# First products of the FFNs: eight column tiles with the tokens stationary, four of them as seven block products for eight

## The chip, the cores and the metric

The kernel runs on one core of a Trainium2 chip. Its engines work side by side: TensorE (in the profile PE, with its weight loads as PEld), VectorE (DVE), ScalarE (ACT), GpSimd (POOL) and SyncE (SP), which issues most transfers. The metric is the device time of one execution in microseconds, smaller being better.

## The reference

A bidirectional encoder trunk of two layers, with 256 tokens of width 1024 in float32. Each layer has a half-step feed-forward network (FFN), a mixer of two kinds of attention, and a second FFN. The change touches the FFNs alone.

```python
SEQ, D_MODEL, D_FF, DEPTH = 256, 1024, 2816, 2

def swiglu(x, w_in, w_out):
    h = x @ w_in
    gate, up = h[..., :D_FF], h[..., D_FF:]
    return (jax.nn.silu(gate) * up) @ w_out

for l in range(DEPTH):
    x = layer_norm(ALPHA * x + 0.5 * swiglu(x, ffn1_w_in[l], ffn1_w_out[l]), ln_g[l, 0], ln_b[l, 0])
    mix = hybrid_mixer(x, ...)
    x = layer_norm(ALPHA * x + mix, ln_g[l, 1], ln_b[l, 1])
    x = layer_norm(ALPHA * x + 0.5 * swiglu(x, ffn2_w_in[l], ffn2_w_out[l]), ln_g[l, 2], ln_b[l, 2])
```

## The kernel before, in words

**Numbers in two halves.** TensorE multiplies in a shortened float32 (fp32r). Each operand is therefore split in a high half (a cast, made on ScalarE: wh, L118) and a low half (the rest, a subtraction on VectorE: wl, L119). A product is then three: high by high, high by low, low by high. All weights come from memory and are split in the kernel. `Weights` does it in the order of a list, `srcs`: a tile of 128 x 1024 is loaded to `raw` (five buffers), and its halves go to `wh` and `wl` (nine buffers each). `W.get(i)` hands out entry i and emits what lies up to nine buffers ahead; that work has a priority of 100 places less (LATER).

**An FFN's first products (x @ w_in).** The width of 2816 is 22 column tiles of 128, each with a gate and an up half. x stands transposed in `xx`, in halves, with its 1024 channels as eight k tiles. Column tiles 0 to 3 (NB = 4) go through `first`: 128 tokens are stationary and 512 columns of weights move past them, for two token tiles, eight k tiles, three parts and two halves (gate, up): 96 matmuls of 512 columns (L381). Its results have the tokens on partitions; `first_t` (L397) transposes them with four TensorE transposes for each token tile, and splits them (L401, L402). The other 18 tiles go through `col`: the weights are stationary and all 256 tokens move, high and low half side by side, so for each half of a tile 8 "wide" matmuls of 512 columns (L419) with wh and 8 "narrow" ones of 256 (L424) with wl. ScalarE and VectorE then add the two parts of a bank (L434, L435), apply Silu (L436), multiply (L438) and split the product (L441, L442) into the tiles `gs`. Tiles come in twos; with `flip` the narrow matmuls go first.

**The second products.** The 22 row tiles of w_out are taken as "o" (one row tile, 12 matmuls, `step`, L503) or "S" (two row tiles as a block pair, `pair`, L527): 2 x 2 blocks are multiplied with seven products instead of eight, by sums of blocks (Winograd's form). The weight sums of a pair are made on VectorE in `_make_pair` (four operations, L86 to L89, before the splits, L72 and L73), those of the activations in `sums` (L457 to L462). `STR` names the five pairs, PLAN the order, and the last seven single tiles come at the end.

**Order.** TensorE's order is the order in which the program emits. The other engines' orders, and the buffers, are set by a scheduler when the kernel is built, by priority and its own estimate of times. PSUM has eight banks, all under one tag `b`.

**Stages in the profile.** FFNs begin at about 4.8, 283.3, 464.2 and 742.7 us; the mixers lie between the first and the second, and between the third and the fourth.

Of the kernel before, what the change touches and what calls it, by code (L numbers as in the profile page):

```python
# [19 lines left out]
P = 128  # L20
# [34 lines left out]
0; P sq 1 1; V 1; O 0 2; T sq 1; O 0 2; B 0 0; S s 1; B 0 1; Y 1; W 0 0; W 0 1; S s 1; O 1 1; O 0 1; O 1 1; O 0  # L55
3; B 1 0; B 1 1; W 1 0; W 1 1; O 1 2; Z; O 1 4
"""


class Weights:  # L60
# [15 lines left out]
    def _make_pair(self, i):  # L76


        nc, dv = self.nc, self.nc.vector
        r0, r1, ta = (self.pool.tile([P, 1024], F32, tag="raw", name=f"raw{i}{c}", bufs=5) for c in "abt")  # L80
        for r, src in zip((r0, r1), self.srcs[i][1:]):
            nc.sync.dma_start(r, src)
        t4 = self.tmp.tile([P, 512], F32, tag="tmp", name=f"t4_{i}")
        a, b = slice(0, 512), slice(512, 1024)
        with self.tc.high_priority(-LATER):
            dv.tensor_tensor(ta[:, a], r0[:, b], r0[:, a], ALU.subtract)  # L86
            dv.tensor_tensor(ta[:, b], r0[:, b], r1[:, b], ALU.add)
            dv.tensor_tensor(r0[:, b], r1[:, b], ta[:, a], ALU.add)
            dv.tensor_tensor(t4, r1[:, a], r0[:, b], ALU.subtract)  # L89
# [9 lines left out]
    def _make(self, i):  # L99
        nc = self.nc  # L100
        if self.srcs[i][0] == "S":
            return self._make_pair(i)
        raw = self.pool.tile([P, 1024], F32, tag="raw", name=f"raw{i}", bufs=5)
        wh = self.pool.tile([P, 1024], F32R, tag="wh", name=f"wh{i}", bufs=9)
        wl = self.pool.tile([P, 1024], F32R, tag="wl", name=f"wl{i}", bufs=9)

        n = 512 if i < 3 else 1024
        src = self.srcs[i]

        rows = src if isinstance(src, tuple) else (src,)  # L110
        for c in range(0, 1024, n):
            s = slice(c, c + n)
            for q, r in enumerate(rows):
                h = P // len(rows)

                (nc.sync if i or c else nc.scalar).dma_start(raw[q * h : (q + 1) * h, s], r[:, s])
            with self.tc.high_priority(0 if i < 3 else -LATER):
                nc.scalar.copy(wh[:, s], raw[:, s])  # L118
                nc.vector.tensor_tensor(wl[:, s], raw[:, s], wh[:, s].bitcast(F32), ALU.subtract)  # L119
        self.made.append((wh, wl))  # L120
# [15 lines left out]
def encoder_kernel(  # L136
# [44 lines left out]
    def out_rows(w):  # L181
        row = lambda k: w[k * P : (k + 1) * P, :]
        rows = [row(k) if u == "o" else ("S", row(2 * k), row(2 * k + 1)) for u, k in plan]
        return rows + [row(k) for k in tail]

    srcs = []
    for l in range(DEPTH):
        srcs += [f1_b[l, k] for k in range(KT)]
        srcs += [f1_in[l, j, s] for j in range(JT - NB) for s in range(2)]
# [9 lines left out]
        srcs += [f2_b[l, k] for k in range(KT)]  # L199
        srcs += [f2_in[l, j, s] for j in range(JT - NB) for s in range(2)]  # L200
        srcs += out_rows(f2_out[l])
    W = Weights(tc, wp, tp, srcs)
    wi = 0
# [113 lines left out]
        nc.sync.dma_start(bt, ln_b[l, n].partition_broadcast(P))  # L317
        return gt, bt

    def to_xt(src, t, nm, hs=(0, 1), gain=None):  # L320

        with tc.high_priority():
            for h in hs:
                tr = ps.tile([P, 4, P], F32, tag="b", name=f"tr_{nm}{t}{h}")
                for i in range(4):
                    c = (4 * h + i) * P
                    nc.tensor.transpose(tr[:, i, :], src[:, c : c + P], ident)
                dh = xx[:, 4 * h : 4 * h + 4, 0, t, :]
                dl = xx[:, 4 * h : 4 * h + 4, 1, t, :]
                if gain is None:  # L330
                    nc.scalar.copy(dh, tr)
                    dv.tensor_tensor(dl, tr, dh.bitcast(F32), ALU.subtract)
                else:
                    nc.scalar.mul(dh, tr, gain)
                    dv.scalar_tensor_tensor(dl, tr, gain, dh.bitcast(F32), ALU.mult, ALU.subtract)
# [25 lines left out]
    def ffn(l, n, last=False):  # L361
        nonlocal wi
        nm = f"{l}{n}"
        gs = [gp.tile([P, 2, 2, SEQ], F32R, tag="g", name=f"g_{nm}_{q}") for q in range(JT // 2)]

        def first(ts, mid=None):

# [23 lines left out]
                out.append(gv)  # L391
            return out

        def first_t(gv, t):
            tr = ps.tile([P, 4, P], F32, tag="b", name=f"trg_{nm}{t}")
            for i in range(4):
                nc.tensor.transpose(tr[:, i, :], gv[:, i * P : (i + 1) * P], ident)  # L397
            for q in range(2):
                a = slice(t * P, (t + 1) * P)
                dh = gs[q][:, :, 0, a]  # L400
                nc.scalar.copy(dh, tr[:, 2 * q : 2 * q + 2, :])  # L401
                dv.tensor_tensor(gs[q][:, :, 1, a], tr[:, 2 * q : 2 * q + 2, :], dh.bitcast(F32), ALU.subtract)  # L402

        def col(*js, flip=False):

            nonlocal wi
            ts = []
            for j in js:

                hs = [ps.tile([P, 2, SEQ], F32, tag="b", name=f"h{'gu'[s]}_{nm}_{j}") for s in range(2)]  # L410
# [5 lines left out]
            def wide(hs, ws, s):  # L416
                for k in range(KT):

                    mm(hs[s], ws[s][0][:, k * P : (k + 1) * P], xx[:, k], start=(k == 0 and not flip),  # L419
                       stop=(k == KT - 1 and flip), skip_group_check=flip)  # L420

            def narrow(hs, ws, s):
                for k in range(KT):
                    mm(hs[s][:, 1, :], ws[s][1][:, k * P : (k + 1) * P], xx[:, k, 0], start=(k == 0 and flip),  # L424
                       stop=(k == KT - 1 and not flip), skip_group_check=flip)

            one, two = (narrow, wide) if flip else (wide, narrow)
            for j, hs, tl, ws in ts:
                for s in range(2):
                    one(hs, ws, s)  # L430
            for j, hs, tl, ws in ts:
                for s in range(2):
                    two(hs, ws, s)
                    nc.scalar.copy(tl[:, s], hs[s][:, 1, :])  # L434
                    dv.tensor_tensor(tl[:, s], hs[s][:, 0, :], tl[:, s], ALU.add)  # L435
                nc.scalar.activation(tl[:, 0], tl[:, 0], AF.Silu)  # L436
                gv = tl[:, 1]
                dv.tensor_tensor(gv, tl[:, 0], gv, ALU.mult)  # L438
                q, jj = divmod(j, 2)
                n = P if q in STR and jj == 0 else SEQ  # L440
                nc.scalar.copy(gs[q][:, jj, 0, 0:n], gv[:, 0:n])  # L441
                dv.tensor_tensor(gs[q][:, jj, 1, 0:n], gv[:, 0:n], gs[q][:, jj, 0, 0:n].bitcast(F32), ALU.subtract)  # L442
                if q in STR and jj:
                    sums(q, ts[0][2][:, 1], gv)

        sm = {}

# [18 lines left out]
        if first_x:  # L466
            g0, g1 = first((0, 1))
        else:
            (g0,) = first((0,), lambda: to_xt(x[1], 1, f"x{nm}"))
            (g1,) = first((1,))  # L470
        wi += KT
        if not first_x:
# [89 lines left out]
        todo += [(i, [c]) for c in fin for i in range(TAIL - SPLIT, TAIL)]  # L562
        for n_, (i, cs) in enumerate(todo):
            if n_ == len(todo) - TCUT and not last:
                to_xt(x[0], 0, f"y{nm}")
# [18 lines left out]
    def mixer(l):  # L584
# [263 lines left out]
        for tok in ORDER.split(";"):  # L848
# [37 lines left out]
            elif op == "X":  # L886
                to_xt(x[1], 1, f"m{l}")
            elif op == "Z":
                to_xt(x[0], 0, f"z{l}")
            elif op == "S":  # L890
                do_s(*ar)
            elif op == "A":
# [89 lines left out]
```

## Time and profile before

| | |
|---|---|
| median of 3 runs | 931.92 us (931.63 to 932.51) |
| the profiled execution's own time | 931.88 us |
| its span in the profile | 930.1 us |
| granted TensorE clock, mean | 0.997 |
| PE busy | 922.0 us (99%), 4970 instructions |
| DVE busy | 789.5 us (85%), 1344 instructions |
| ACT busy | 569.1 us (61%), 970 instructions |
| HBM read | 174.35 MB, 189 GB/s over the span |

The span goes from the first to the last instruction that the profile counts. Busy is the share of the span in which an engine executes. The profile can be asked for the chain of work that ended last (followed back from the last instruction), for the busy time in chosen stretches, and for the instructions in order of time (start, duration, engine, line, operation, out<-in with sizes, count, and in brackets the idle time before with what ended it).

### The profile page before, as it was taken

Reading aid. Unit: us, or ns where it says so; the run is one execution under the profiler, and the core shown is the slowest. Engines: PE = TensorE matmul, PEld = TensorE weight load, DVE = VectorE, ACT = ScalarE, POOL = GpSimd, SP = SyncE. Lnnn points to the kernel's source line nnn. Section 1 sums busy time; section 2 is a strip of 40 time slices with the busy share of each in tenths; the row PEclk is TensorE's granted clock in tenths of the full one; section 3 lists DMA queues with packets and bytes.
Section 4 is the critical chain, followed back from the end, with each engine's and each line's share of the span. In section 5 each row is a group of like instructions: output and inputs, shape, how many; then the busy total and the mean of one; then the engine's idle time right before and its main releaser. Section 6 shows DMA issues by size and latency. Waiting matters only on the chain.

```text
span 930.1 us, 13767 instructions
## 1 busy us (share of the span) xinstructions
PE 922.0 (99%) x4970; PEld 788.2 (85%) x4970; DVE 789.5 (85%) x1344; ACT 569.1 (61%) x970; POOL 17.0 (2%) x27
## 2 busy tenths in 40 slices
PE   9999999999999999999999999999999999999996
PEld 7888888888888888888888888888888889888885
DVE  7898899998987678899986888999988976888896
ACT  5768656546865666656546666663478656666650
POOL 0000000000000000000000000000000000000000
PEclk9999999999999999999999999999999999999998
DMA  9986546675426755547675665575844365665551
GB/s 315 310 271 202 159 145 218 226 248 152 125 90 206 245 181 181 161 154 218 224 254 191 187 194 162 158 254 175 275 112 137 107 228 188 193 190 159 159 180 46
DMA packets 51379, 176.29 MB, mean 190 GB/s; under 512 B 6512, under 2 KB 8304, under 8 KB 51312
## 3 DMA queue, kind: packets, MB, share of 16 engines
q1 hardware_dynamic: 51024, 175.03, 58.7%
q8 instruction: 39, 0.64, 0.3%
q10 hardware_dynamic: 288, 0.39, 0.1%
q14 instruction: 28, 0.23, 0.1%
HBM read 174.35 MB, written 1.05 MB: 189 GB/s over the span
## 4 chain that ended last, share of the span: by engine, by line
PE 99%; DVE 1%; issue 0%; DVEq 0%
PE hg L419 14%; PE hu L419 14%; PE acc L503 14%; PE hb L381 9%; PE hu L424 7%; PE hg L424 7%; PE pp L527 6%; PE ao L840 5%; PE acc L527 4%; PE os L776 1%; PE pj_sq L619 1%; PE pj_sq L617 1%; PE pj_dv L617 1%; PE pj_sq L618 1%; PE pj_dq L617 1%; PE pj_dv L619 1%
## 5 line engine op out<-in xcount | busy, mean ns | idle before, releaser
L119 DVE TENSOR_TENSOR wl<-raw,wh 128x1024 fp32r<-128x1024 f32 (+1 forms) x279 | 336.1, 1210 | 73.7 <-PE hg L424 28.8
L118 ACT CAST wh<-raw 128x1024 fp32r<-128x1024 f32 (+1 forms) x279 | 290.6, 1047 | 117.4 <-PE acc L503 29.3
L419 PE MATMUL hg<-xx,wh 128*128 128x512 f32 x576 | 143.2, 391 | 0.0
L419 PE MATMUL hu<-xx,wh 128*128 128x512 f32 x576 | 142.3, 389 | 0.0
L419 PEld LDWEIGHTS hu<-xx,wh 128*128 128x128 f32 x576 | 108.1, 188 | 22.5
L419 PEld LDWEIGHTS hg<-xx,wh 128*128 128x128 f32 x576 | 106.6, 188 | 21.2
L503 PE MATMUL acc<-wh,g 128*128 128x512 f32 (+1 forms) x390 | 109.0, 387 | 0.0
L503 PEld LDWEIGHTS acc<-wh,g 128*128 128x128 f32 x390 | 72.9, 188 | 14.7
L424 PE MATMUL hg<-xx,wl 128*128 128x256 f32 x576 | 81.0, 283 | 0.0
L424 PE MATMUL hu<-xx,wl 128*128 128x256 f32 x576 | 80.9, 283 | 0.0
L424 PEld LDWEIGHTS hg<-xx,wl 128*128 128x128 f32 x576 | 75.4, 192 | 1.6
L424 PEld LDWEIGHTS hu<-xx,wl 128*128 128x128 f32 x576 | 74.3, 192 | 0.0
L381 PE MATMUL hb<-wh,xx 128*128 128x512 f32 x256 | 70.3, 395 | 0.0
L503 PE MATMUL acc<-wl,g 128*128 128x512 f32 (+1 forms) x195 | 61.6, 386 | 0.0
L381 PEld LDWEIGHTS hb<-wh,xx 128*128 128x128 f32 x256 | 48.3, 190 | 10.5 <-ACT wh L118 0.6
L434 ACT COPY tl<-hg 128x256 f32<-128x256 f32 x72 | 26.8, 372 | 32.0 <-PE hg L419 28.1
L503 PEld LDWEIGHTS acc<-wl,g 128*128 128x128 f32 x195 | 36.6, 188 | 7.3
L434 ACT COPY tl<-hu 128x256 f32<-128x256 f32 x72 | 26.8, 372 | 20.2 <-PE hu L424 17.1
L381 PE MATMUL hb<-wl,xx 128*128 128x512 f32 x128 | 38.9, 391 | 0.0
L840 PE MATMUL ao<-wh,xx 128*128 128x512 f32 x128 | 37.0, 398 | 0.0
L441 ACT CAST g<-tl 128x128 fp32r<-128x128 f32 (+1 forms) x72 | 27.1, 376 | 15.9 <-DVE tl L438 14.0
L436 ACT ACTIVATE tl<-tl 128x256 f32<-128x256 f32 x72 | 30.2, 419 | 6.5 <-DVE tl L435 5.6
(972 smaller groups left out, 1477.4 us busy)
## 6 DMA issues: line engine op xcount, KB each, us to landing
raw<-in_f_in_dram SPq DMA_DIRECT2D x144, 512.0 KB, 4.4
raw<-in_f_out_dram SPq DMA_DIRECT2D x48, 512.0 KB, 4.1
raw<-in_m_in_dram SPq DMA_DIRECT2D x36, 512.0 KB, 4.7
raw<-in_f_b_dram SPq DMA_DIRECT2D x29, 512.0 KB, 4.3
raw<-in_m_out_dram SPq DMA_DIRECT2D x8, 512.0 KB, 4.7
raw<-in_m_out_dram SPq DMA_DIRECT2D x16, 256.0 KB, 4.4
lng<-in_ln_g_dram SPq DMA_DIRECT2D x6, 512.0 KB, 4.9
lnb<-in_ln_b_dram SPq DMA_DIRECT2D x6, 512.0 KB, 6.0
```

Of the source, the lines that this page charges most:

```text
L118: nc.scalar.copy(wh[:, s], raw[:, s])
L119: nc.vector.tensor_tensor(wl[:, s], raw[:, s], wh[:, s].bitcast(F32), ALU.subtract)
L381: mm(hb[s], xx[:, k, g, t, :], ww[:, 512 * s : 512 * s + 512], start=(k == 0 and e == 0), stop=(k == KT - 1 and e == 2))
L419: mm(hs[s], ws[s][0][:, k * P : (k + 1) * P], xx[:, k], start=(k == 0 and not flip), stop=(k == KT - 1 and flip), skip_group_check=flip)
L424: mm(hs[s][:, 1, :], ws[s][1][:, k * P : (k + 1) * P], xx[:, k, 0], start=(k == 0 and flip), stop=(k == KT - 1 and not flip), skip_group_c ...
L434: nc.scalar.copy(tl[:, s], hs[s][:, 1, :])
L436: nc.scalar.activation(tl[:, 0], tl[:, 0], AF.Silu)
L441: nc.scalar.copy(gs[q][:, jj, 0, 0:n], gv[:, 0:n])
L503: mm(a, g, ww[:, s], start=(k == ka and e == 0), stop=(k == kb and e == 2))
L527: mm(o, g, ww, start=(own and first and e == 0), stop=(own and final and e == 2))
L617: mm(o, xx[:, k, 0, t, :], wh[:, s], start=(k == 0), stop=False)
L840: mm(acc[t][h], xx[:, k, g, t, :], ww[:, s], start=(k == 0 and e == 0), stop=(k == KT - 1 and e == 2))
```

## The change

NB goes from 4 to 8: column tiles 0 to 7 now have the tokens stationary. Tiles 0 to 3 (NF = 4) go through `first` as before. Tiles 4 to 7 go through the new `group`: two token tiles by two k tiles as 2 x 2 blocks, four such pairs of k tiles, seven products for each pair, each product in three parts, in seven banks: 84 matmuls of 512 columns. For it

- the weight tiles of the four pairs are made by `_make_pair` (through `S` entries in `srcs`, `in_rows`);
- x is needed unsplit: `to_xt` copies it to `xkeep` (on ScalarE, with a priority of KEEP = 20 places less), and the first FFN loads it from memory; `x_sums` makes four sums on VectorE and splits them;
- after each of the first three pairs, and after the banks are gathered, one half of the ordinary tiles 9 and 10 is computed (`by_halves`); tile 8 comes before the group through `col`;
- the seven banks are gathered to two results with VectorE and ScalarE, and `first_t` transposes these after column tile 11.

The pairs of the second products become 6 to 10 instead of 3 to 7. The tiles `gs` are allocated one by one. The loading of x and the rotary tables, in the first FFN, come after tiles 12 and 13 instead of 6 and 7. The weights of the first eight column tiles are laid out as 2048 columns for each k tile, of which an entry takes 512 gate and 512 up columns.

```diff
-NB = 4
+NF = 4
+KEEP = 20
+NB = 8
-STR = (3, 4, 5, 6, 7)
+STR = (6, 7, 8, 9, 10)
...
+    def in_rows(b, w):
+        blk = lambda g, k: b[k].rearrange("p (s g c) -> p g s c", s=2, g=NB // NF)[:, g]
+        cols = [w[j, s] for j in range(JT - NB) for s in range(2)]
+        mid = [u for k in range(KT // 2) for u in (("S", blk(1, 2 * k), blk(1, 2 * k + 1)), cols[2 + k])]
+        return [blk(0, k) for k in range(KT)] + cols[:2] + mid + cols[2 + KT // 2 :]
...
-    def to_xt(src, t, nm, hs=(0, 1), gain=None):
+    xkeep = {}
+
+    def to_xt(src, t, nm, hs=(0, 1), gain=None, keep=False):
...
+                    if keep:
+                        with tc.high_priority(-KEEP):
+                            nc.scalar.copy(xkeep[t][:, 4 * h : 4 * h + 4, :], tr)
...
+        def by_halves(*js):
+            nonlocal wi
+            for j in js:
+                tl = tp.tile([P, 2, SEQ], F32, tag="tl", name=f"tl_{nm}_{j}", bufs=2)
+                for s in range(2):
+                    h, w = bank(j, s), W.get(wi)
+                    wi += 1
+                    wide(h, w, False)
+                    narrow(h, w, False)
+                    gather(h, tl, s)
+                    if s:
+                        gated(j, tl)
+                    yield
...
+        def split(src, nm_):
+            s = gp.tile([P, 2, 4, P], F32R, tag="g", name=f"sx_{nm}_{nm_}")
+            nc.scalar.copy(s[:, 0], src)
+            dv.tensor_tensor(s[:, 1], src, s[:, 0].bitcast(F32), ALU.subtract)
+            return s
+
+        def x_sums():
+            v = [xkeep[t].rearrange("p (k e) c -> p k e c", e=2) for t in range(2)]
+            a11, a12, a21, a22 = v[0][:, :, 0], v[0][:, :, 1], v[1][:, :, 0], v[1][:, :, 1]
...
+            dv.tensor_tensor(s1, a21, a22, ALU.subtract)
...
+            dv.tensor_tensor(s4, a12, s2, ALU.subtract)
+            out.append(split(s4, 4))
+            return out
+
+        def group(xs, between):
+            nonlocal wi
+            b = {c: ps.tile([P, 512], F32, tag="b", name=f"pg_{nm}_{c}") for c in range(1, 8)}
+            for k in range(KT // 2):
+                b11, b21, b22, t4, t1, t2, t3 = W.get(wi)
+                wi += 1
...
+                for c in (2, 3, 5, 7, 1, 6, 4) if k < KT // 2 - 1 else (1, 2, 6, 7, 5, 3, 4):
+                    (ah, al), (bh, bl) = what[c]
+                    for e, (a_, w_) in enumerate(((ah, bh), (ah, bl), (al, bh))):
+                        mm(b[c], a_, w_, start=(k == 0 and e == 0), stop=(k == KT // 2 - 1 and e == 2))
+                if k < KT // 2 - 1:
+                    next(between)
...
+            nc.scalar.copy(v, b[1])
+            add(g0, b[2], v)
+            nc.scalar.activation(g0, g0, AF.Silu)
+            add(v, b[6], v)
+            add(w, b[7], v)
+            add(v, b[5], v)
+            add(u1, b[5], w)
+            add(v, b[3], v)
+            dv.tensor_tensor(v, g0, v, ALU.mult)
+            add(w, b[4], w)
+            nc.scalar.activation(w, w, AF.Silu)
+            dv.tensor_tensor(w, w, u1, ALU.mult)
+            next(between)
+            return v, w
...
+        if first_x:
+            for t in range(2):
+                xkeep[t] = gp.tile([P, KT, P], F32, tag="g", name=f"xf_{nm}{t}")
+                nc.sync.dma_start(xkeep[t], x_tr[:, t])
+        else:
             first_t(g0, 0)
+        xs = x_sums()
         col(NB)
...
-        for j in (NB + 1, *range(NB + 2, JT, 2)):
-
-            col(*((j,) if j == NB + 1 else (j, j + 1)), flip=(j % 4 == 0 or j == NB + 1))
-            if first_x and j == NB + 2:
+        ga, gb_ = group(xs, by_halves(NB + 1, NB + 2))
+        for j in (NB + 3, *range(NB + 4, JT, 2)):
+
+            col(*((j,) if j == NB + 3 else (j, j + 1)), flip=(j % 4 == 2 or j == NB + 3))
+            if j == NB + 3:
+                first_t(ga, 0, NF // 2)
+                first_t(gb_, 1, NF // 2)
+            if first_x and j == NB + 4:
```

More of the change, by code (lines that the diff above doesn't have):

```diff
@@ L57, with _cols @@
 """
+def _cols(t, like):
+    return t if len(like.shape) == 2 else t.rearrange("p (s c) -> p s c", s=like.shape[1])
 class Weights:
@@ L114, in _make @@
                 h = P // len(rows)
-                (nc.sync if i or c else nc.scalar).dma_start(raw[q * h : (q + 1) * h, s], r[:, s])
+                dst = _cols(raw[q * h : (q + 1) * h], r)
+                s_ = s if len(r.shape) == 2 else slice(c // 512, (c + n) // 512)
+                (nc.sync if i or c else nc.scalar).dma_start(dst[:, s_], r[:, s_])
             with self.tc.high_priority(0 if i < 3 else -LATER):
@@ L198, in encoder_kernel @@
                  for n in range(KT // 2)]
-        srcs += [f2_b[l, k] for k in range(KT)]
-        srcs += [f2_in[l, j, s] for j in range(JT - NB) for s in range(2)]
+        srcs += in_rows(f2_b[l], f2_in[l])
         srcs += out_rows(f2_out[l])
@@ L363, in ffn, with g_tiles @@
         nm = f"{l}{n}"
-        gs = [gp.tile([P, 2, 2, SEQ], F32R, tag="g", name=f"g_{nm}_{q}") for q in range(JT // 2)]
+        gs = {}
+        def g_tiles(*qs):
+            for q in qs:
+                gs[q] = gp.tile([P, 2, 2, SEQ], F32R, tag="g", name=f"g_{nm}_{q}")
         def first(ts, mid=None):
@@ L392, in first, with first_t @@
             return out
-        def first_t(gv, t):
-            tr = ps.tile([P, 4, P], F32, tag="b", name=f"trg_{nm}{t}")
+        def first_t(gv, t, q0=0):
+            if not t:
+                g_tiles(q0, q0 + 1)
+            tr = ps.tile([P, 4, P], F32, tag="b", name=f"trg_{nm}{t}{q0}")
             for i in range(4):
@@ L399, in first_t, with wide, narrow, gather @@
                 a = slice(t * P, (t + 1) * P)
-                dh = gs[q][:, :, 0, a]
+                dh = gs[q0 + q][:, :, 0, a]
                 nc.scalar.copy(dh, tr[:, 2 * q : 2 * q + 2, :])
-                dv.tensor_tensor(gs[q][:, :, 1, a], tr[:, 2 * q : 2 * q + 2, :], dh.bitcast(F32), ALU.subtract)
+                dv.tensor_tensor(gs[q0 + q][:, :, 1, a], tr[:, 2 * q : 2 * q + 2, :], dh.bitcast(F32), ALU.subtract)
+        def wide(h, w, flip):
+            for k in range(KT):
+                mm(h, w[0][:, k * P : (k + 1) * P], xx[:, k], start=(k == 0 and not flip),
+                   stop=(k == KT - 1 and flip), skip_group_check=flip)
+        def narrow(h, w, flip):
+            for k in range(KT):
+                mm(h[:, 1, :], w[1][:, k * P : (k + 1) * P], xx[:, k, 0], start=(k == 0 and flip),
+                   stop=(k == KT - 1 and not flip), skip_group_check=flip)
+        def gather(h, tl, s):
+            nc.scalar.copy(tl[:, s], h[:, 1, :])
+            dv.tensor_tensor(tl[:, s], h[:, 0, :], tl[:, s], ALU.add)
+        def gated(j, tl, prev=None):
+            nc.scalar.activation(tl[:, 0], tl[:, 0], AF.Silu)
+            gv = tl[:, 1]
+            dv.tensor_tensor(gv, tl[:, 0], gv, ALU.mult)
+            q, jj = divmod(j, 2)
+            if not jj:
+                g_tiles(q)
+            n = P if q in STR and jj == 0 else SEQ
+            nc.scalar.copy(gs[q][:, jj, 0, 0:n], gv[:, 0:n])
+            dv.tensor_tensor(gs[q][:, jj, 1, 0:n], gv[:, 0:n], gs[q][:, jj, 0, 0:n].bitcast(F32), ALU.subtract)
+            if q in STR and jj:
+                sums(q, prev[:, 1], gv)
+        def bank(j, s):
+            return ps.tile([P, 2, SEQ], F32, tag="b", name=f"h{'gu'[s]}_{nm}_{j}")
+        def by_halves(*js):
[11 more added lines that the diff above has]
+                    yield
         def col(*js, flip=False):
@@ L408, in col @@
             for j in js:
-                hs = [ps.tile([P, 2, SEQ], F32, tag="b", name=f"h{'gu'[s]}_{nm}_{j}") for s in range(2)]
+                hs = [bank(j, s) for s in range(2)]
                 tl = tp.tile([P, 2, SEQ], F32, tag="tl", name=f"tl_{nm}_{j}", bufs=2)
@@ L414, in col @@
                 ts.append((j, hs, tl, ws))
[L416 to L425, printed above, removed]
             one, two = (narrow, wide) if flip else (wide, narrow)
@@ L429, in col @@
                 for s in range(2):
-                    one(hs, ws, s)
+                    one(hs[s], ws[s], flip)
             for j, hs, tl, ws in ts:
                 for s in range(2):
[L433 to L444, printed above, removed]
+                    two(hs[s], ws[s], flip)
+                    gather(hs[s], tl, s)
+                gated(j, tl, ts[0][2])
+        def split(src, nm_):
[3 more added lines that the diff above has]
+            return s
@@ L468, in ffn @@
         else:
[L469 removed]
+            (g0,) = first((0,), lambda: to_xt(x[1], 1, f"x{nm}", keep=True))
             (g1,) = first((1,))
         wi += KT
[L472 removed]
+        if first_x:
+            for t in range(2):
+                xkeep[t] = gp.tile([P, KT, P], F32, tag="g", name=f"xf_{nm}{t}")
+                nc.sync.dma_start(xkeep[t], x_tr[:, t])
+        else:
             first_t(g0, 0)
+        xs = x_sums()
         col(NB)
```

27 lines of the change are left out of this document (22 added, 5 removed).

## The prediction

> **What bounds the kernel now.** I read the page's busy shares and its chain first, then the busy time by stage, then the chain and VectorE's timeline around the first products.
>
> ```profile
> PE 922.0 (99%) x4970; PEld 788.2 (85%) x4970; DVE 789.5 (85%) x1344; ACT 569.1 (61%) x970; POOL 17.0 (2%) x27
> PE 99%; DVE 1%; issue 0%; DVEq 0%
> ```
>
> TensorE is busy for 99% of the span, and the chain that ends last is 99% TensorE: a matmul less is time less, as long as what feeds TensorE keeps up. VectorE is next, with 85%. The shares by stage tell more (the columns: stretch and length, then busy us and count for PE, PEld, DVE, ACT and POOL, granted clock, DMA share, GB/s):
>
> ```profile
> 4.77:27.57 22.80, 22.80 (x98) 18.80 (x98) 18.64 (x25) 13.96 (x17) 0.00 (x0) 1.00 0.99 352
> 283.31:306.42 23.11, 23.11 (x109) 19.24 (x109) 17.13 (x22) 11.80 (x14) 1.00 (x1) 1.00 0.67 221
> 306.42:340.00 33.58, 33.58 (x196) 29.80 (x196) 24.23 (x43) 21.17 (x40) 0.00 (x0) 1.00 0.62 203
> 340.00:406.83 66.83, 66.83 (x386) 59.25 (x386) 55.42 (x102) 43.31 (x78) 0.00 (x0) 1.00 0.55 167
> 406.83:444.23 37.40, 37.40 (x167) 30.97 (x166) 34.35 (x39) 23.32 (x27) 0.00 (x0) 1.00 0.67 210
> ```
>
> The three middle rows are the first products of the second FFN: 123.5 us, in which VectorE works 17.13 + 24.23 + 55.42 = 96.8 us (78%) and ScalarE 76.3 us (62%). The last row is its second products with the five block pairs, where VectorE is at 92% and TensorE still never waits. The first row is the start of the first FFN, where the DMA engines are at 0.99. So the change is to be weighed on two accounts: what TensorE saves, and whether VectorE's slack of 26.7 us in those 123.5 us covers what it is given.
>
> **TensorE's account.** From the chain (start, length, what):
>
> ```profile
> 33.11 0.87 PE trg L397 x8
> 54.48 1.84 PE hg L419 x8
> 76.69 1.84 PE hg L419 x8
> 413.63 2.72 PE pp L527 x12
> 438.79 2.04 PE acc L527 x9
> 487.30 1.85 PE hg L419 x8
> 492.90 0.44 PE trg L397 x4
> ```
>
> Four ordinary column tiles go from 54.48 to 76.69, 22.21 us, so a half (gate or up of one tile) is 2.78 us. Their replacement is 4 pairs x 7 products x 3 = 84 matmuls of 512 columns. Such matmuls run at 2.72 / 12 = 0.2267 us each in the block pairs of the second products, so 19.04 us, one pair being 4.76. Two more sets of four transposes, 0.44 each, add 0.88. Net: 22.21 - 19.04 - 0.88 = 2.29 us saved in each FFN, 9.2 us in four. The eight tiles that now go tokens-stationary replace nothing else: first() keeps its 96 matmuls, and the two tiles that are split into halves run the same 32 each.
>
> **VectorE's account.** Its records overlap, so I price an operation by the distance between starts:
>
> ```profile
> 397.14 0.42 DVE L438 TENSOR_TENSOR tl<-tl 128x256 f32<-128x256 f32 x1
> 397.48 1.22 DVE L73 TENSOR_TENSOR wl133t<-raw133t,wh133t 128x1024 fp32r<-128x1024 f32 x1
> 428.16 0.69 DVE L86 TENSOR_TENSOR raw140t<-raw140a 128x512 f32<-128x512 f32 x1
> 428.76 0.69 DVE L73 TENSOR_TENSOR wl139f<-t,wh139f 128x512 fp32r<-128x512 f32 x1
> 429.36 0.69 DVE L87 TENSOR_TENSOR raw140t<-raw140a,raw140b 128x512 f32<-128x512 f32 x1
> 430.69 1.22 DVE L73 TENSOR_TENSOR wl140b<-raw140b,wh140b 128x1024 fp32r<-128x1024 f32 x1
> 431.82 0.68 DVE L89 TENSOR_TENSOR t<-raw140b,raw140a 128x512 f32<-128x512 f32 x1
> 511.71 0.28 DVE L459 TENSOR_TENSOR sf<-tl 128x128 f32<-128x128 f32 x1
> 511.91 0.28 DVE L457 TENSOR_TENSOR sf<-tl,tl 128x128 f32<-128x128 f32 x1
> ```
>
> 512 columns cost 0.605 us, 1024 cost 1.135, 256 cost 0.335, 128 cost 0.20. Removed in each FFN: 8 low halves of weights (9.1) and four tiles' two adds, product and subtraction (16 x 0.335 = 5.4), 14.5 in all. Added: 4 weight pairs, each five operations of 512 and three of 1024 = 6.43 (25.7); the x sums, four and their four low halves (4.8); the nine operations that gather the seven banks (5.4); four subtractions behind the new transposes (1.3): 37.3. Net +22.8 us in each FFN. The stage's account becomes 119.6 us of VectorE in 121.2 us of TensorE. Over the run VectorE goes from 789.5 to about 881 us, 95% of 923.
>
> [...]
>
> ```profile
> L118 ACT CAST wh<-raw 128x1024 fp32r<-128x1024 f32 (+1 forms) x279 | 290.6, 1047 | 117.4 <-PE acc L503 29.3
> ```
>
> ScalarE: the casts of a pair are three of 1024 and one of 512 against two of 1024 before, with x splits, x copies and two Silu; at 1.05 us per 1024 that is some 9 us on 76.3, 70%. It stays off the path. The x copies sit behind the casts of xx; the two loads of x for the first FFN move 1 MB, 3.0 us at 352 GB/s, on the sync queue behind weights. Weight rows in pieces of half the length: no row prices it; between 0 and the 1.05 us by which the first 96 matmuls (22.80) already exceed 96 x 0.2267. I take 0, as the rows after the start show DMA shares of 0.55 to 0.67. The moved block pairs of the second products, the tiles allocated late and the later rotary work cost TensorE nothing by themselves.
>
> **Where the slack is not.** An average of 119.6 in 121.2 us says little, since only nine weight buffers let VectorE run ahead. So I follow it from the point where it is first free for the new work:
>
> ```profile
> 18.53 6.35 DVE L119 TENSOR_TENSOR wl<-raw,wh 128x1024 fp32r<-128x1024 f32 x5
> 412.24 0.69 DVE L87 TENSOR_TENSOR raw137t<-raw137a,raw137b 128x512 f32<-128x512 f32 x1 [0.33 <-DMA raw137b<-in_f_out_dram]
> 421.68 0.69 DVE L87 TENSOR_TENSOR raw139t<-raw139a,raw139b 128x512 f32<-128x512 f32 x1 [0.50 <-DMA raw139b<-in_f_out_dram]
> 473.44 1.29 DVE L332 TENSOR_TENSOR xx<-tr_x,xx 128x512 fp32r<-128x512 f32 x2
> 476.42 0.69 DVE L390 TENSOR_TENSOR gvb<-sgb,hb 128x512 f32<-128x512 f32 x1 [1.68 <-ACT sgb L388]
> 507.19 1.23 DVE L119 TENSOR_TENSOR wl<-raw,wh 128x1024 fp32r<-128x1024 f32 x1 [5.23 <-issue]
> ```
>
> In a later FFN (the third) it is free at 474.7, with the eight rows' weights made. The group starts after the first column tile and g1's transposes, at 492.90 + 0.44 = 493.3. Ahead of it stand: two gate products 1.2, x sums 4.8, one column half 1.1, pair 0 6.4, eight operations of 256 for transposes and that tile 2.7, the next half 1.1: 17.4. The last pair begins three times (4.76 + 2.78) = 22.6 us into the group, at 515.9, and at once wants all but the last piece of its weights; for that VectorE needs pairs 1 and 2, two halves, 5.8 of pair 3 and the gathering of three halves, 22.6. It arrives at 474.7 + 40.0 = 514.7: 1.2 us early. Column tile 11 starts with the low halves of its weights, the second due at 515.9 + 7.54 + 0.95 = 524.4; by then come 10.5 more (the gathering of the banks 5.4, three weights 3.4, pair 3's rest and one half 1.6), until 525.2: 0.8 late, without a moment idle. The bank gathering is emitted ahead of those weights, so I let it go first.
>
> VectorE is not without idle time even when it is the busy one: 0.33 and 0.50 us before each pair's second row of weights, 8% in the stage of 37.40 us. On 50 us I allow 0 to 4 per cent, 0 to 2 us: late by 0.8 to 2.8, taken in the middle, 1.8, in each of three FFNs.
>
> In the first FFN it is free later relative to TensorE: the five operations from 18.53 end at 24.9, the last being for a weight that now comes after the pair, so 23.75. The DMA engines, full until 27.57, allow nothing earlier. The group would start at 33.11 + 0.87 = 34.0. Its work ahead is 16.3 (no first column halves), so the last pair's weights are ready at 23.75 + 38.9 = 62.7 against 56.6, 6.1 late; tile 11's at 73.1 against 65.1, 8.0 late. I take the middle, 7.0.
>
> Sum against the profiled execution, 931.88 us (0.04 below the median of the runs): -9.2 + 7.0 + 3 x 1.8 = +3.2, so 935.1. What is late next: nothing behind tile 11, where an ordinary tile needs two low halves, four operations of 256 and half a set of sums, 4.3 us of VectorE in 22.21 / 4 = 5.55, and it catches up.
>
> **The rivals.** First, on the other side: *the cover holds*. Place: the gathering of the banks against tile 11's weights. For it: 5.23 us in which VectorE stood still in the third FFN (507.19) and 1.68 before 476.42, and several counted operations that TensorE doesn't need yet (gatings, late transposes, some 2 us). If the weights go ahead of the gathering, only the last pair decides: it is early in three FFNs and 6.1 late in the first, 931.9 - 9.2 + 6.1 = 928.8; with everything hidden 922.7. It decides as soon as all stalls together stay under 9.2 us. Against it: the first FFN, where VectorE has hardly a gap.
>
> Second: *the backlog reaches the second products*. The last block pair there starts at 438.79 + 3 x 0.2267 = 439.5 and its first weights were done at 431.9, 7.6 us ahead. Three more sets of sums now fall into the last tiles (four operations of 128 columns and one of 512, 1.4 us each set), leaving 3.3. An arrears above that stops TensorE again, some 2 us in each FFN: 943.
>
> [...]
>
> **How the numbers follow.** About 0.2%, 1.9 us, is what a measurement here can tell from no change. VectorE late as summed, 933.8 to 942: 0.40. The cover holds, below 930: 0.37. Stalls that just eat the gain, 930 to 933.8: 0.17. The backlog in the second products or the slow clock: 0.06. So faster 0.37, same 0.17, slower 0.46. The predicted time is 935.1. The range leaves out full hiding at its low end and 943 and more at its high end: 925.5 to 942; the forecast's own is 933.8 to 942.
>
> **What would show it.** Matmuls of the group at 0.227 us where they run; VectorE's share near 95% overall and with almost no idle time from the second row of first() to tile 11; TensorE waiting on a weight's low half in the last pair or at tile 11, longest in the first FFN; no wait in the second products. I am wrong if TensorE stays without gaps in the group (then 922.7), or if the waits stand before the group, on the x sums or a bank.

## The result, and the profile after

The change makes the kernel slower: 947.82 us (median; 946.65 to 950.26) against 931.91 us, a ratio of 1.0175 (95% interval 1.0162 to 1.0187). The forecast was 935.1 with a range to 942.0: the sign is right, the size is not. The profiled execution took 946.83 us, and on it the rest of this section rests. Its page begins:

```profile
span 945.0 us, 13662 instructions
...
PE 922.1 (98%) x4826; PEld 778.7 (82%) x4826; DVE 868.2 (92%) x1460; ACT 593.5 (63%) x994; POOL 17.0 (2%) x27
...
PE 78%; DVE 13%; DMA 5%; ACT 2%; issue 2%; SPq 0%; DVEq 0%; ACTq 0%
```

TensorE has 144 instructions less and is busy just as long: its matmuls take longer somewhere. The chain, which was TensorE for 99%, now goes through VectorE for 13%. The chain also gives the borders of the stages (start, length, what): the first products of an FFN begin with `hb`, its second products with `acc` x24. In the chain of the kernel before, the second FFN begins at 283.31, and the third has:

```profile
464.19 8.17 PE hb L381 x36
...
587.72 5.44 PE acc L503 x24
```

The chain of the kernel after, with the second FFN's begin and the third's group:

```profile
294.09 8.16 PE hb L405 x36
...
475.39 8.17 PE hb L405 x36
...
508.07 5.54 PE pg L535 x16
...
516.39 4.79 PE pg L535 x21
...
601.02 5.47 PE acc L622 x24
```

From the one start to the other, the first products of the three later FFNs took 123.52, 123.53 and 123.53 us before; after, 123.92, 125.63 and 125.39. The second FFN begins 10.78 us later. Together 10.78 + 0.40 + 2.10 + 1.86 = 15.1 us. The row at 508.07 shows one reason: 16 matmuls in 5.54 us, where the whole pairs run 21 in 4.79 (0.228 each, as forecast). The waits of PEld in the changed kernel (us in total, times, longest), without those that the kernel before has too:

```profile
PEld pg L535 <- ACT sx L498: 10.0, 4, 3.1
PEld tr_y L343 <- DVE x L374: 2.8, 2, 2.6
...
PEld pg L535 <- DVE wl16a L79: 2.2, 1, 2.2
...
PEld pg L535 <- ACT wh16a L78: 1.6, 1, 1.6
```

`sx` are the split x sums: TensorE waits for them at the start of the group in all four FFNs (for 2.72, 1.85, 1.95 and 1.71 us on its own timeline, PE). Only in the first FFN does it wait for the last pair's weights (16a). Nothing waits at column tile 11.

The slow matmuls are seen in stretches laid behind these waits (stretch, length, busy us and count of PE, PEld, DVE, ACT and POOL, granted clock, DMA share, GB/s), in the changed kernel:

```profile
38.30:41.70 3.40, 3.37 (x8) 2.67 (x9) 3.40 (x8) 1.65 (x5) 0.00 (x0) 0.53 0.40 146
65.40:68.80 3.40, 3.40 (x8) 2.72 (x9) 2.48 (x4) 1.88 (x4) 0.00 (x0) 0.50 0.87 288
327.00:330.40 3.40, 3.40 (x16) 2.81 (x15) 3.40 (x7) 2.84 (x5) 0.00 (x0) 1.00 0.00 0
509.10:512.50 3.40, 3.40 (x9) 2.63 (x8) 3.40 (x6) 2.87 (x4) 0.00 (x0) 0.50 0.03 6
```

The stretches are the first FFN's group start and last pair, and the group starts of the second and third. In three of these four (0.53, 0.50 and 0.50), and in the fourth FFN (0.57 from 789.5 us), the clock is granted at half for about 3.4 us, and 8 to 10 matmuls run where 16 do at full clock; each time some 1.7 us are lost, an estimate from these rows (half of 3.4). Behind the wait of the second FFN it stays at 1.00.

Three of the waits ahead of such stretches, and in the third row one more wait, on the timeline of TensorE in the changed kernel (in brackets the idle time before and what ended it):

```profile
37.45 0.50 PE L535 MATMUL pg<-wh10b,sx 128*128 128x512 f32 x1 [2.72 <-ACT sx L498]
...
65.36 0.79 PE L535 MATMUL pg<-wl16a,xx 128*128 128x512 f32 x1 [1.88 <-DVE wl16a L79]
...
193.09 1.32 PE L343 MATMUL tr_y<-ident,x 128*128 128x128 f32 x8 [2.13 <-DVE x L374]
...
507.18 0.50 PE L535 MATMUL pg<-wh150b,sx 128*128 128x512 f32 x1 [1.95 <-ACT sx L498]
```

The third row is a wait that the forecast didn't have: behind the first FFN's second products, the transposes of the layer norm's result. Behind it the clock stays at 1.00 (193.00 to 197.80 us). Ahead of the second row TensorE had already waited 1.41 us for the same pair's high half, with three matmuls in between.

### The profile page after: what moved, and what is told of

Same layout as the page of the kernel before. It is cut to its first block, busy times and chain, and to the rows that moved or that the text cites. A ratio compares the mean times of both kernels' runs of the same rounds, so it can differ in the third digit from the quotient of the medians.

```text
span 945.0 us, 13662 instructions
## 1 busy us (share of the span) xinstructions
PE 922.1 (98%) x4826; PEld 778.7 (82%) x4826; DVE 868.2 (92%) x1460; ACT 593.5 (63%) x994; POOL 17.0 (2%) x27
## 4 chain that ended last, share of the span: by engine, by line
PE 78%; DVE 13%; DMA 5%; ACT 2%; issue 2%; SPq 0%; DVEq 0%; ACTq 0%
PE acc L622 10%; PE pg L535 8%; PE hg L432 8%; PE hu L432 8%; PE hb L405 5%; PE ao L959 5%; PE pp L646 4%; PE hu L437 4%; PE hg L437 4%; PE acc L646 3%; DVE wl L127 2%; DMA raw<-in_f_out_dram 1%; DVE sx L499 1%; DMA raw<-in_f_b_dram 1%; PE os L895 1%
## 5 line engine op out<-in xcount | busy, mean ns | idle before, releaser
L126 ACT CAST wh<-raw 128x1024 fp32r<-128x1024 f32 (+1 forms) x247 | 255.8, 1045 | 98.8 <-DMA raw<-in_f_in_dram 27.0
L127 DVE TENSOR_TENSOR wl<-raw,wh 128x1024 fp32r<-128x1024 f32 (+1 forms) x247 | 294.0, 1203 | 16.7 <-ACT wh L126 9.6
L432 PE MATMUL hg<-xx,wh 128*128 128x512 f32 x448 | 111.8, 391 | 0.0
L432 PE MATMUL hu<-xx,wh 128*128 128x512 f32 x448 | 110.7, 389 | 0.0
L432 PEld LDWEIGHTS hu<-xx,wh 128*128 128x128 f32 x448 | 84.1, 188 | 17.6
L432 PEld LDWEIGHTS hg<-xx,wh 128*128 128x128 f32 x448 | 82.8, 188 | 16.4
L437 PE MATMUL hg<-xx,wl 128*128 128x256 f32 x448 | 62.7, 283 | 0.0
L452 ACT CAST g<-tl 128x256 fp32r<-128x256 f32 (+1 forms) x56 | 20.5, 366 | 19.6 <-DVE tl L447 19.1
L405 PEld LDWEIGHTS hb<-wl,xx 128*128 128x128 f32 x128 | 23.9, 188 | 5.2 <-DVE wl L127 0.2
L959 PEld LDWEIGHTS ao<-wh,xx 128*128 128x128 f32 x128 | 23.3, 188 | 5.4 <-issue 0.8
```

What stands on the lines that cost most here:

```text
L405: mm(hb[s], xx[:, k, g, t, :], ww[:, 512 * s : 512 * s + 512], start=(k == 0 and e == 0), stop=(k == KT - 1 and e == 2))
L432: mm(h, w[0][:, k * P : (k + 1) * P], xx[:, k], start=(k == 0 and not flip), stop=(k == KT - 1 and flip), skip_group_check=flip)
L437: mm(h[:, 1, :], w[1][:, k * P : (k + 1) * P], xx[:, k, 0], start=(k == 0 and flip), stop=(k == KT - 1 and not flip), skip_group_check=flip)
L959: mm(acc[t][h], xx[:, k, g, t, :], ww[:, s], start=(k == 0 and e == 0), stop=(k == KT - 1 and e == 2))
```

## Why the x sums were late: order or capacity

VectorE's timeline in the third FFN of the changed kernel, from where x stands split to the last x sum:

```profile
485.96 0.68 DVE L92 TENSOR_TENSOR raw150t<-raw150a 128x512 f32<-128x512 f32 x1
...
496.91 0.69 DVE L93 TENSOR_TENSOR raw152t<-raw152a,raw152b 128x512 f32<-128x512 f32 x1 [0.68 <-DMA raw152b<-in_f_b_dram]
...
499.25 1.22 DVE L79 TENSOR_TENSOR wl152b<-raw152b,wh152b 128x1024 fp32r<-128x1024 f32 x1
500.39 0.68 DVE L414 TENSOR_TENSOR gvb<-sgb,hb 128x512 f32<-128x512 f32 x1
...
501.32 0.68 DVE L509 TENSOR_TENSOR xs<-xf_x 128x512 f32<-128x512 f32 x1
...
507.33 0.68 DVE L499 TENSOR_TENSOR sx<-xs,sx 128x512 fp32r<-128x512 f32 x1
```

Their inputs, two copies on ScalarE, are there at about 486.7 (485.48 + 1.18). VectorE then makes pair 0's weights (150), which the group needs from its start as it needs the sums, but ahead of the last sum also five operations for pair 1's (152), 4.1 us by the forecast's prices, which TensorE wants only one pair later (from 516.39). It reaches the first sum only behind the second gate product. Two theories. *Order*: the sums stand too late in VectorE's queue, and put earlier they cost nothing, since the work fits. *Capacity*: VectorE is full, and what is put earlier makes something else late. They share TensorE's saving and differ in what is left when the order is mended.

**xs_early** gives the order alone, in the three later FFNs:

```diff
             (g0,) = first((0,), lambda: to_xt(x[1], 1, f"x{nm}", keep=True))
+            xs = x_sums()
             (g1,) = first((1,))
...
-        xs = x_sums()
+        if first_x: xs = x_sums()
```

> The changed kernel (947.8 us) with x_sums written between the two halves of first() in the three later FFNs, so that VectorE makes the x sums some 10 us sooner; the first FFN is left as it is. Theory A (order): the group waits because the x sums stand behind pair 0's weights and half of pair 1's on VectorE, and nothing else is late; the three later FFNs then lose their 2.7, 4.4 and 4.2 us: 936 to 938. Theory B (capacity): VectorE has no time left, and what is made later instead, the last pair's weights, is now late by about as much: the wait moves there, 944 to 948.

Measured: 934.27 us, 1.0031 (1.0022 to 1.0041) of the kernel before. One line moved is worth 13.5 us of the 15.9. By the chains of the two profiled executions, 13.0 us apart, 10.9 of them lie in the three later FFNs. The other 2.1 lie in the first FFN, whose program is the same: its group start keeps the clock at 1.00 here, behind a wait of 2.05 us instead of 2.72, and that is not what the moved line was meant to do. The chain of this kernel, third FFN:

```profile
470.73 8.17 PE hb L405 x36
...
522.55 4.79 PE pg L535 x21
...
592.07 5.47 PE acc L623 x24
```

And its VectorE on the timeline:

```profile
484.45 0.68 DVE L509 TENSOR_TENSOR xs<-xf_x 128x512 f32<-128x512 f32 x1
...
490.95 0.68 DVE L499 TENSOR_TENSOR sx<-xs,sx 128x512 fp32r<-128x512 f32 x1
...
520.25 1.22 DVE L79 TENSOR_TENSOR wl156a<-raw156a,wh156a 128x1024 fp32r<-128x1024 f32 x1
521.99 2.35 DVE L127 TENSOR_TENSOR wl<-raw,wh 128x1024 fp32r<-128x1024 f32 x2
524.59 0.68 DVE L539 TENSOR_TENSOR gr_g<-pg,gr_v 128x512 f32<-128x512 f32 x1
525.19 1.21 DVE L127 TENSOR_TENSOR wl<-raw,wh 128x1024 fp32r<-128x1024 f32 x1
```

592.07 - 470.73 = 121.34 us (121.37 and 121.37 in the other two): with no wait left, the change saves 2.16 us in each FFN. So in the later FFNs it was order. But the capacity is nearly used up, as the forecast's ledger had it: the last pair's last low half (wl156a) is done at 521.47 and its pair begins at 522.55, 1.1 us early, and VectorE's busy time in the stretch around the group is 98% (columns as above):

```profile
480.00:534.00 54.00, 54.00 (x274) 45.96 (x273) 53.08 (x75) 38.35 (x56) 0.00 (x0) 1.00 0.59 200
```

**early_load** tests that margin: xs_early with the first x sum made seven times over, six operations more at 0.6 us, 3.6 us of VectorE ahead of the group in each later FFN.

```diff
-            dv.tensor_tensor(s1, a21, a22, ALU.subtract)
+            for _ in range(1 if first_x else 7): dv.tensor_tensor(s1, a21, a22, ALU.subtract)
```

> The run with early sums (934.3 us) with the first x sum made seven times instead of once in the three later FFNs: 3.6 us more work for VectorE, nothing else. Theory A (VectorE is at its limit in the group: its last weights for the last pair came 1.0 us ahead there, and it stood still nowhere): 2.6 us late in each, 942, and up to 1.7 more for each time the clock drops. Theory B (there is slack left that the trace doesn't show, in what is made early): 934 to 936.

Measured: 945.67 us, 1.0158 (1.0139 to 1.0177), 11.4 more than xs_early. In each of the three FFNs TensorE now waits for the last pair's weights, 1.9 us each time, and some 0.8 us for the gate product, which xs_early does not show (PEld's waits):

```profile
PEld trg L423 <- DVE gvb L414: 2.4, 3, 0.9
...
PEld pg L535 <- DVE wl156a L79: 1.9, 1, 1.9
```

That is 1.9 + 0.8 = 2.7 us in each FFN. A margin of 1.1 us leaves 3.6 - 1.1 = 2.5 of the added work uncovered, so the size fits. In one of the three there is also a stretch of slow clock behind it (granted 0.61 from 346.70 to 350.10 us). By the chain the three stages lose 4.7, 3.1 and 3.2 us, the first being the one with the slow clock.

**What holds the sums back.** The scheduler goes by priority, yet the copies were ready 15 us before the first sum. Two runs ask whether it is the priority or the buffers. xs_priority raises the sums' priority where they stand; xs_own_buffers takes the four sums' buffers from the pool of x instead of the `tmp` buffers that the gate products also use, and leaves priority and place alone.

```diff
-        xs = x_sums()
+        with tc.high_priority(): xs = x_sums()
```

> The changed kernel with the highest priority for x_sums, at its place. Theory A (buffers in the order of the program): the sums still come behind the second gate product and only pass one weight of pair 1 and one transposed half, 1.1 to 1.5 us less waiting in each later FFN, and 1.7 us for each slow clock that goes with it: 940 to 945. Theory B (rank): all waits at the group's start go, 936 as with early sums.

```diff
-            f = lambda c: tp.tile([P, 4, P], F32, tag="tmp", name=f"xs_{nm}_{c}")
+            fs = [xp.tile([P, 2, 4, P], F32, tag="x", name=f"xs_{nm}_{c}") for c in range(2)]; f = lambda c: fs[(c - 1) // 2][:, (c - 1) % 2]
```

> The changed kernel with x_sums where the change has it, but its four sums in two tiles of the pool of x instead of four of the pool that first()'s Silu and gate product also use. Theory A (a tile is given its buffer only after those that stand ahead of it in the program and share its pool; the sums waited for the second gate product for that reason alone): the four sums move up by some 10 us without any priority, their low halves stay behind (they share a pool with the tiles of the first transposes), and 4 x 0.605 = 2.4 us of the wait go in the three later FFNs, with the slow clock: 937 to 941. Theory B (they stand late because of the weights' rank): nothing moves, 946 to 949.

Measured: with priority 942.30 us, 1.0114 (1.0100 to 1.0128); with the other buffers 936.67, 1.0054 (1.0040 to 1.0068). The raised priority takes the wait away in no FFN: it is shorter in the second and the third (1.95 to 1.03 us in the third, with the clock at 1.00 behind it) and longer in the first and the fourth (2.72 to 3.24, 1.71 to 2.38); in all, 5.5 us less than the change. TensorE's timeline, third FFN:

```profile
505.55 0.50 PE L535 MATMUL pg<-wh150b,sx 128*128 128x512 f32 x1 [1.03 <-ACT sx L498]
```

Even so the first sum starts behind the second gate product (500.21, after 499.62). The other buffers move them, without any priority, 12 us ahead of it (VectorE's timeline, third FFN):

```profile
484.58 0.68 DVE L509 TENSOR_TENSOR xs<-xf_x 128x512 f32<-128x512 f32 x1
...
496.56 0.69 DVE L414 TENSOR_TENSOR gvb<-sgb,hb 128x512 f32<-128x512 f32 x1
...
498.56 2.50 DVE L499 TENSOR_TENSOR sx<-xs,sx 128x512 fp32r<-128x512 f32 x4
```

In that FFN no wait is left: its first products take 121.33 us (594.25 - 472.92); the second and the fourth take 122.9 and 121.8. The low halves `sx` stay behind the gate product: their buffers are still of the pool `g`, which `first_t` asks earlier in the program. So it is buffers: the run shows that those of `tmp` held the sums back. That a pool hands its buffers out in the order in which the program asks, and that the sums asked behind the second token tile's gate product, is the explanation that fits this run and xs_early, where the same `tmp` buffers were asked for earlier. For `g` no run tests it.

## The clock after a wait

**filler** leaves every wait and gives TensorE something to do in it: small matmuls on constants in front of the group's second product, into a bank that is begun anew behind them. They take somewhat longer than the wait (by the chain 2.42 us for 1.95 in the third FFN).

```diff
+                    if k == 0 and c == 3:
+                        for _ in range(14 if first_x else 11):
+                            mm(b[c], one(1.0, [P, P], BF16), one(1.0, [P, 512], BF16), start=True, stop=True)
```

> The changed kernel with matmuls that nobody needs (11, in the first FFN 14, of 512 columns, bfloat16) put into the bank of the group's second product ahead of its first matmul, so that TensorE works where it waited. Theory A (the wait is followed by some 3.4 us at half clock, 1.7 us lost in three of the four FFNs): 947.8 - 5 = 943, and the granted clock stays at 1.0 behind the group's start. Theory B (the slow matmuls there have another cause, such as late operands): no gain, 948 to 950.

Measured: 944.83 us, 1.0142 (1.0127 to 1.0157), 3.0 us less than the change. The third FFN, with the fillers (first row) and behind them, and the first FFN's last pair (third row), where there are none:

```profile
505.90:508.40 2.50, 2.50 (x13) 1.28 (x13) 2.50 (x5) 1.82 (x4) 0.00 (x0) 1.00 0.28 106
508.40:512.00 3.60, 3.60 (x18) 2.90 (x17) 3.60 (x9) 2.55 (x5) 0.00 (x0) 1.00 0.02 5
66.00:70.00 4.00, 4.00 (x10) 3.07 (x10) 3.07 (x5) 2.78 (x4) 0.00 (x0) 0.50 0.98 339
```

With work without use in the place of the wait the clock stayed at 1.00: in the first FFN from 36.00 to 42.00 us, in the third over the first two rows, in the fourth from 787.60 to 791.00. In the third and fourth FFN that gave 1.3 us each, the 1.7 less what the fillers last too long; in the second, where the clock had not fallen, 0.1. In the first it gave nothing in the end. The group's start ran at full clock and the second pair began 1.4 us earlier (44.91 instead of 46.31). But at the last pair the two waits together were as long as before (3.29 us), and the half clock behind them lasted longer, granted 0.80 from 60.00 to 66.00 us and 0.50 from 66.00 to 70.00, some 6.4 us at half by these two, where the changed kernel has about 3.4 us of it; the second FFN began 0.8 us later. So the slow clock is a cost of its own, but what one avoided stretch is worth depends on what follows it.

What length of wait is needed, these runs leave open. No single wait of the changed kernel was longer than 2.72 us in PE (3.1 in PEld), and the clock fell behind waits of 1.95 us in the third FFN and 1.71 in the fourth; behind 1.85 us in the second it did not.

## The first FFN

In xs_early the first FFN still costs 8.7 us (the second begins at 291.99 instead of 283.31). The stretch from the end of its `first` to the last pair, in the changed kernel:

```profile
26.20:65.40 39.20, 33.04 (x160) 27.10 (x158) 38.63 (x57) 26.86 (x41) 0.00 (x0) 0.96 0.60 197
```

VectorE is busy for 38.63 of 39.20 us, which speaks for capacity here, not order. So does xs_own_buffers, which moved the sums forward in this FFN too. TensorE's wait for them fell from 2.72 to 0.9 us, but TensorE then waited 1.0 us for the second pair's weights (wl12t) and 3.3 us in all at the last pair, as before, and the FFN still cost 9.4 us. Two runs test it. **no_xs** leaves the x sums out of every FFN, eight operations on VectorE (4.8 us) and four on ScalarE; the group then multiplies unsummed blocks of x, so the kernel no longer computes the FFN. **plain_first** takes the seven products out of the first FFN alone, whose tiles 4 to 7 then go through `first` a second time.

```diff
-                s1, s2, s3, s4 = ([s[:, h, k] for h in range(2)] for s in xs)
+                s1, s2, s3, s4 = blk(0, 1), blk(1, 1), blk(0, 0), blk(1, 0)
...
-        xs = x_sums()
-        ga, gb_ = group(xs, by_halves(NB + 1, NB + 2))
+        ga, gb_ = group(None, by_halves(NB + 1, NB + 2))
```

> The changed kernel without x_sums: the group multiplies unsummed blocks of x where the four sums belong, so this leaves out eight operations of 512 columns on VectorE and four on ScalarE in each FFN; everything else is as in the changed kernel. Theory A (order): the waits at the group's start go in all four FFNs, 11.3 + 5.4 us: 931 or somewhat less. Theory B (capacity): VectorE has 4.8 us less to do in each FFN and still is late for the last pair in some of them: 934 to 940.

```diff
+        if plain:
+            return [blk(g, k) for g in range(2) for k in range(KT)] + cols
...
+            ga, gb_ = first((0, 1), g="2")
+            wi += KT
```

> The changed kernel, but in the first FFN tiles 4 to 7 are computed by a second round of first() with plain products (96 matmuls), without x sums and weight pairs; the other three FFNs keep the group. Theory A (the first FFN loses 10.3 us in its first products and 2.8 in its second by VectorE being late): 947.8 - 12.7 = 935. Theory B (its loss comes from the weight rows in pieces of half the length, or from the start's transfers): it stays, 944 or more.

Measured: no_xs 928.79 us, 0.9962 (0.9950 to 0.9974); plain_first 938.26, 1.0071 (1.0055 to 1.0088). The chain of no_xs at the second FFN:

```profile
286.94 8.16 PE hb L405 x36
...
408.31 5.47 PE acc L621 x24
```

And its waits of PE:

```profile
PE pg L535 <- DVE wl16a L79: 1.6, 1, 1.6
PE tr_y L343 <- DVE x L374: 1.0, 1, 1.0
```

408.31 - 286.94 = 121.37, the saving of 2.16 again. Without the sums the first FFN still waits for its last pair and costs 3.6 us (286.94 against 283.31): the backlog there is larger than the sums. In plain_first all of it is gone (chain):

```profile
129.00 5.47 PE acc L625 x24
...
284.15 8.16 PE hb L407 x36
```

The second FFN begins 0.84 us later than before, and no wait of the group or of `tr_y` is left up to there. So 9.9 of the 10.78 us are the price of the seven products in the first FFN. The run as a whole gains 9.6 us on the change, not the 12.7 expected, and 2.16 of the difference are what the plain products give up of the saving. No other order was tried there than that of xs_own_buffers.

## A version that is faster than both

**both** takes plain_first, and xs_early's place for the sums in the later FFNs.

> x sums written between the two halves of first() in the three later FFNs, and plain products for tiles 4 to 7 in the first FFN. If the two findings are separate, each later FFN takes 121.35 us as in the run with early sums (123.53 before) and the first one 0.84 us more than before, as in the run with plain products: 931.8 - 3 x 2.16 + 0.84 = 926.1. If they disturb each other (the later FFNs were 1.9 us slower in the run with plain products than their kin, by the slow clock), 927 to 930.

Measured: 926.39 us against 931.96 of the kernel before in the same runs, 0.9938 (0.9926 to 0.9950). Its page has:

```profile
PE 915.6 (99%) x4838; PEld 776.8 (84%) x4838; DVE 843.3 (91%) x1421; ACT 579.0 (63%) x980; POOL 17.0 (2%) x27
```

And its chain, third FFN:

```profile
462.77 8.17 PE hb L407 x36
...
584.10 5.47 PE acc L625 x24
```

121.33 us for the first products (121.38 in the second and the fourth), the second FFN beginning 0.7 us later than before, and TensorE at 99% of the span again. Three times 2.16 less 0.7 is 5.8; 5.6 were measured.

## Why the prediction was wrong, point by point

Measured in the forecast's terms, the profiled execution has: 4 x 2.16 = 8.6 us saved (forecast 9.2); 6.9 of waits in the first FFN's first products (7.0), since its second products begin at 136.53 instead of 128.38, 8.15 later, to which the 2.16 are added and from which two slow stretches of 1.7 are taken; 2.5, 2.6 and 2.3 of waits in the later FFNs (1.8 each), the stage less 121.37, less 1.7 where the clock fell; 4 x 1.7 = 6.8 of slow clock (not in the sum); 2.6 behind the first FFN, 10.78 - 8.15 (not in the sum). -8.6 + 6.9 + 7.4 + 6.8 + 2.6 = 15.1.

- **TensorE's account** was right: 2.29 forecast, 2.16 measured. Weight rows of half the length cost nothing that shows: the first ordinary tile begins at the same time, within 0.06 us (27.41 before, 27.47 after, on the two timelines).
- **VectorE's account** was somewhat high: 868.2 us busy for 881. Its 116 instructions more are the 29 that the forecast's list makes for each FFN.
- **The ledger of the last pair** in a later FFN (ready 1.2 us early) was right where the sums are in time: 1.1 in xs_early, and early_load shows that it decides.
- **The failed step: the work ahead of the group.** The forecast asked only whether the 17.4 us ahead of the group fit, and took their order for given. They fit, as xs_early shows, but in the changed kernel the sums came last of them, behind 4.1 us of pair 1's weights that were not yet wanted, and TensorE waited 1.71 to 1.95 us for them in each later FFN, with half clock behind two of the three waits. Its own text named this as the way to be wrong (waits ahead of the group, on the x sums), and gave it no price.
- **Tile 11** (0.8 late, 1.8 with the gaps) was wrong: the weights were made between the operations that gather the banks (521.99, 524.59, 525.19 in xs_early), and no run waits there for weights. The 1.8 us came near to the 2.5 measured by chance, at another place.
- **The first FFN**: 7.0 forecast, 6.9 measured without the clock, and for the reason given, VectorE's capacity, but not in the places given: TensorE waited 2.72 us at the group's start, 3.29 at the last pair (6.1 forecast) and not at all at tile 11 (8.0). That the middle of 6.1 and 8.0 came so near is chance.
- **The slow clock** was the mis-sized term: the forecast gave it a chance, 0.06 together with the second products, and no place in the sum. No run shows how long a wait has to be for it; the runs showed that it came four times in the changed kernel, behind waits of 2.72, 1.88, 1.95 and 1.71 us, 1.7 us each, 6.8 us.
- **The second products**: the backlog did reach behind them, 2.6 us once, in the first FFN, but at the layer norm's transposes (a wait of 2.13 us, 1.0 in no_xs, none in plain_first), where its rival looked at the block pairs' weights.
- **The rival "the cover holds"** fails in the first FFN, which costs 3.6 us even without the sums (no_xs); with the order mended it is what the later FFNs do.

The slow clock's 6.8, the 2.6 behind the first FFN, 0.6 of saving less and 2.0 of later waits more make 12.0; between the forecast and the profiled execution lie 11.7.

## What to carry to other kernels

Where a busy engine has room by the sum of its work, look also at the order in which it will do it: work for later can stand before the small operation with which the next stage begins, and which buffers that operation takes, and where the program asks for them, can fix this more firmly than a priority does. Price a wait of TensorE of about 2 us with the clock that may fall behind it (here 1.7 us each time that it fell, behind four of six waits of 1.71 to 2.72 us). A stage at the start of the program, where nothing was prepared ahead, has its own ledger and may be worth a version of its own.

## What the runs showed of the hardware

In the changed kernel TensorE waited six times for 1.7 us or longer. Behind four of the waits (2.72, 1.88, 1.95 and 1.71 us) the clock was granted at half for about 3.4 us, each time 1.7 us lost; behind the other two (1.85 us at the second FFN's group start, 2.13 us ahead of the layer norm's transposes) it stayed at 1.00. Behind fillers, in the place of a wait, it stayed at 1.00 too, in the first, the third and the fourth FFN of filler. Whether it falls is not fixed by the wait's length alone: it fell behind 1.71 us and stayed behind 2.13. plain_first, whose later FFNs are those of the change, waits for the x sums at the group's start in each of them (6.5 us in all, 2.4 the longest) and shows either outcome there, in the third FFN and in the second; the stretches behind the two waits (columns as above, the clock third from the end):

```profile
501.00:504.50 3.50, 3.50 (x17) 2.92 (x16) 3.50 (x7) 3.10 (x5) 0.00 (x0) 1.00 0.01 2
317.00:320.50 3.50, 3.35 (x10) 2.59 (x10) 3.50 (x8) 2.40 (x6) 0.00 (x0) 0.64 0.00 0
```

Their first products took 123.92 and 126.05 us. Nothing here tells what else decides it. It also differs from one execution to the next, and the time with it: those of the changed kernel took 946.65, 946.83, 948.80 and 950.26 us at mean clocks of 0.993, 0.991, 0.990 and 0.988.
